# A two-layer hybrid encoder on one core: the second pair of differential heads moved to the end of the attention

## The chip, the core and the metric

The kernel runs on one NeuronCore of one Trainium2 chip. Its time is the device time of one execution in microseconds (us), and the number to be predicted is the median over several executions. TensorE (PE in the profile) multiplies matrices into eight PSUM banks; VectorE (DVE), ScalarE (ACT) and GpSimd (POOL) do everything else on tiles, and SyncE's queue (SP) starts all transfers. Each engine works through its own instructions strictly in the order in which the program lists them and waits where an operand isn't ready.

## What is computed

The reference, cut to one layer (512 tokens, width 1024, two layers, all in float32):

```python
for l in range(DEPTH):
    x = x + 0.5 * swiglu(rms_norm(x, ffn1_norm[l]), ...)
    h = rms_norm(x, mix_norm[l])
    pa, pb, pc, pd = jnp.split(h @ w_in[l], IN_SPLITS, axis=-1)
    ya = neighbourhood_mixer(pa, ...)   # 4 heads; a query sees 256 or 384 of the 512 keys here
    yb = mla_mixer(pb, ...)             # 4 heads behind two latent projections
    yc = diff_mixer(pc, ...)            # 4 heads, each softmax(1) - lam * softmax(2), plus T5 bias
    yd = gqa_mixer(pd, ...)             # 4 heads on 2 pairs of keys and values
    x = x + jnp.concatenate([ya, yb, yc, yd], axis=-1) @ w_out[l]
    x = x + 0.5 * swiglu(rms_norm(x, ffn2_norm[l]), ...)
    x = rms_norm(x, final_norm[l])
```

## The kernel before

Everything is kept transposed: 128 channels on the partitions, 512 tokens along a row. Every matrix product is done in three passes on numbers split into a high and a low part (`mm3`), so that one 128x128 block of weights against 512 tokens is three matmuls of 128x512. A layer is the first feed-forward block, the attention stage (`mix`), and the second feed-forward block.

In `mix` each group of heads (A neighbourhood, B latent, C differential, D grouped) has a projection (`proj_a`, `proj_b`, `proj_c`, `proj_d`; C and A in two halves "c0", "c1" and "a0", "a1", D in "d0" and "d1"), and its heads' attention is cut into steps of 128 queries, 64 steps a layer. A step writes score tiles into PSUM (one tile, or two in group C, whose heads have two softmaxes: 80 tiles a layer), reads each on DVE with the bias or for its maximum, takes the exponential on ACT, is transposed on TensorE back into PSUM, split on ACT and DVE, and every second step multiplies with the values. Scores alternate between two banks (ring "sc"), transposes between two others ("tr"), one bank collects values ("po"), and projections share two ("mm"). So score tile k+2 can't be written before DVE has read tile k.

After the last step of a group `finish` normalises its outputs and `commit` splits them into two of the eight tiles `xh`, `xl`. `out_proj` multiplies six of these with the output weights (18 matmuls for each of eight row blocks d, and one split of a 128x768 weight piece and one addition to `x[d]` on DVE), and what the last group adds follows in `out_proj_a`, six matmuls for each d. The order of steps is the list `units`; between steps a `Filler` hands out projection and output work in portions (`PACE`).

That order is only the input of a planner: `Plan.issue` takes all recorded operations, simulates them with costs and dependences (and with DVE and GpSimd operations that use their common port held apart), and sorts every engine's instructions by the start times that it found. All instructions therefore carry line L216 in the profile, and tiles must tell them apart: `bank` is PSUM, `round` and `plain` are two large arenas in SBUF, `kr` holds the identity and selection matrices, `x` the running sum.

Of the kernel before, what the change touches and what calls it, by code (L numbers as in the profile page):

```python
# [13 lines left out]
F32R = mybir.dt.float32r  # L14
# [6 lines left out]
P = 128  # L21
T = 512
# [6 lines left out]
ROWS = T // GRID_W  # L29

BANKS = {"mm": 2, "st": 1, "po": 1, "sc": 2, "tr": 2}
PACE = {"c0": 2.5, "c1": 2.5, "d0": 3.0, "d1": 3.0, "b": 3.0, "a0": 1.0, "a1": 1.0}

G_F1, G_MIX, G_F2, G_FIN = 0, 8, 16, 24
G_NAQ, G_NAK, G_NAB = 32, 33, 34
# [184 lines left out]
def tile_encoder(ctx: ExitStack, tc: tile.TileContext, xT, wf, wd, win, wout, wuq, wukv, gains, lamp, rpb, t5,  # L220
# [23 lines left out]
    def area(dt, at, n, rows=P):  # L244
        return arenas[dt][:rows, at:at + n]

    xh, xl = ([area(F32R, (at + 12 * T + k * T) if k < 2 else (k - 2) * T + off, T) for k in range(KD)]
              for at, off in ((32 * T, 0), (34 * T, 6 * T)))  # L250

    def krs(off, n, rows=P):
        return kr[:rows, off:off + n]
# [34 lines left out]
    def bank(tag):  # L288
        return rings[tag].take()
# [40 lines left out]
    def mm3(o, wh, wl, ah, al, first, last):  # L330
        TE.matmul(o, wh, ah, start=first, stop=False)
        TE.matmul(o, wh, al, start=False, stop=False)
        TE.matmul(o, wl, ah, start=False, stop=last)
# [3 lines left out]
    for i, tag in enumerate(("whi", "wlo")):  # L337
        rings[tag] = Ring([area(F32R, 48 * T + (2 * i + j) * 1024, 1024) for j in range(2)])

    def pieces(l):  # L340

        for i in range(20):
            yield win[l, (0, 1, 2, 3, 4, 5, 6, 8, 9, 7, 10, 11, 12, 13, 14, 15, 16, 17, 18, 19)[i]], 1024, G
            if i == 13:
                yield wuq[l], 768, G
                yield wukv[l], 512, G
        for d in range(KD):
            yield wout[l, d, :, 256:1024], 768, V
        for d in range(0, KD, 4):
            yield wout[l, d:d + 4, :, 0:256].rearrange("d p c -> p d c"), 1024, V  # L350
# [526 lines left out]
    def mix(l):  # L877
# [21 lines left out]
        def ring(tag):  # L899
            return mr[tag].take()  # L900
# [125 lines left out]
        class Group:  # L1026
# [7 lines left out]

            def head(self, h, o):
                if self.ys[h // 2] is None:
                    self.ys[h // 2] = ring("qf") if self.g == 0 else x[2 * (self.g - 1) + 1 + h // 2]
                t = ring("hs")
                S.copy(t[:64], o[64:128])
                r = 64 * (h % 2)  # L1040
                V.tensor_tensor(out=self.ys[h // 2][r:r + 64], in0=o[:64], in1=t[:64], op=ALU.add)
# [42 lines left out]

        def out_proj():

            for d in range(KD):
                hi, lo = weight()
                o = bank("mm")
                for i, k in enumerate((4, 5, 6, 7, 2, 3)):  # L1090
                    c = (k - 2) * P
                    mm3(o, hi[:, c:c + P], lo[:, c:c + P], xh[k], xl[k], i == 0, i == 5)
                    if i % 2:
                        yield 1.3
                DMA.dma_start(x[d], xd[d])
                V.tensor_tensor(out=x[d], in0=x[d], in1=o, op=ALU.add)
                yield 0.0

        def out_proj_a(ws):
            for d in (0, 4, 1, 5, 2, 6, 3, 7):  # L1100
                hi, lo = ws[d // 4]
                o = bank("ff")
                for k in range(2):
                    c = (d % 4 * 2 + k) * P
                    mm3(o, hi[:, c:c + P], lo[:, c:c + P], xh[k], xl[k], k == 0, k == 1)
                V.tensor_tensor(out=x[d], in0=x[d], in1=o, op=ALU.add)

        def transpose_p(pt_h, pt_l, p, col, nkt):
# [447 lines left out]
        def call(fn, *a):  # L1556
# [1 line left out]
            yield 0.6  # L1558

        units = [  # L1560
            ("c0", steps_c(C, 0, lambda: done["c0"])), ("c1", steps_c(C, 1, lambda: done["c1"])),
            ("d0", steps_d(Dg, 0, keep, lambda: done["d0"])), ("d1", steps_d(Dg, 1, keep, lambda: done["d1"])),
            ("b", steps_b(B, 0, lambda: done["b"])), ("b", steps_b(B, 1, lambda: done["b"])),
            ("a0", steps_a(A, 0, lambda: done["a0"])), ("a1", steps_a(A, 1, lambda: done["a1"])),
        ]
        ends = {15: (C, [gcs, gcs], True), 31: (Dg, [gcol(l, G_DB), gcol(l, G_DB + 1)], False),
                47: (B, [gcol(l, G_BB), gcol(l, G_BB + 1)], False), 63: (A, [gcol(l, G_NAB), gcol(l, G_NAB + 1)], False)}
        for name, gen in (("c0", proj_c(0, "sc")), ("c1", proj_c(1)), ("d0", proj_d(0, keep)), ("d1", proj_d(1, keep)), ("b", proj_b()),
                          ("a0", proj_a(0)), ("a1", proj_a(1))):
            fill.add(name, gen)  # L1570
        flat = [(u, st) for u, sts in units for st in sts]
        n = len(flat)
# [10 lines left out]
        for k in range(n + 1):  # L1583
            if k + 1 < n:
                flat[k + 1][1].soft()
            if k + 2 < n:
                begin(k + 2)
            if k < n:
                flat[k][1].trans()
            if k:  # L1590
                flat[k - 1][1].values()
                if k - 1 in ends:
                    g, beta, sub = ends[k - 1]
                    urgent.append((g, g.finish(beta, sub)))
            for it in list(urgent):
                more = next(it[1], "end")
                if more == "end":
                    urgent.remove(it)
                    if it[0] is not A:
                        fill.add("commit", call(it[0].commit))  # L1600
                    if it[0] is B:
                        fill.add("out", out_proj())
            if k < n:
                fill.run(PACE[flat[k][0]])
# [1 line left out]
            for _ in it[1]:  # L1606
                pass
        fill.until("out")
        A.commit()
        ws = [weight(), weight()]  # L1610
        ahead_ffn(l, 1)
        out_proj_a(ws)

    def start():

# [67 lines left out]
def _layout(inputs):  # L1683
    g = {k: np.asarray(v) for k, v in inputs.items()}
    L = g["w_in"].shape[0]
    xT = np.ascontiguousarray(g["x"][0].T.reshape(KD, P, T).transpose(1, 0, 2))
    wf, wd, win, wout, wuq, wukv, gains = [], [], [], [], [], [], []
    for l in range(L):
        f_, d_ = [], []
        for n in (1, 2):  # L1690
            a, b = _pieces(g[f"ffn{n}_w_gate"][l], P), _pieces(g[f"ffn{n}_w_up"][l], P)
            f_.append(np.stack([a, b], 1).reshape(-1, P, D))
            d_.append(_pieces(g[f"ffn{n}_w_down"][l], P))
        wf.append(np.stack(f_))
        wd.append(np.stack(d_))
        w = g["w_in"][l]
        A, B, C, Dg = w[:, :768], w[:, 768:1184], w[:, 1184:1952], w[:, 1952:]
        halves = [[m[:, 256 * i + P * p:256 * i + P * p + P] for p in range(2) for i in range(3)] for m in (C, A)]
        order = np.concatenate(halves[0] + [Dg, B[:, :384]] + [B[:, 384:]] * 4 + halves[1], axis=1)
        win.append(_pieces(order, P))  # L1700
        wout.append(_pieces(g["w_out"][l], P))
        q = g["mla_w_uq"][l].reshape(256, 4, 96)
        q = np.concatenate([q[:, :, :64].reshape(256, 256), q[:, :, 64:].reshape(256, 128)], axis=1)
        wuq.append(q.reshape(2, P, 384).transpose(1, 0, 2).reshape(P, 768))
        kv = g["mla_w_ukv"][l].reshape(128, 4, 128)
        wukv.append(np.concatenate([kv[:, :, :64].reshape(128, 256), kv[:, :, 64:].reshape(128, 256)], axis=1))

        def col(a):
            return a[l].reshape(-1, P).T

        def rep(a, n):
            return np.concatenate([a] * n)[:, None]

        q, k = g["mla_q_norm"][l], g["mla_k_norm"][l]
        gains.append(np.concatenate([
            col(g["ffn1_norm"]), col(g["mix_norm"]), col(g["ffn2_norm"]), col(g["final_norm"]),
            rep(g["na_q_norm"][l], 2), rep(g["na_k_norm"][l], 2), col(g["na_beta"]),
            col(g["mla_q_lat_norm"]), col(g["mla_kv_lat_norm"]),
            rep(q[:64], 2), rep(q[64:], 4), rep(k[:64], 2), rep(k[64:], 4), col(g["mla_beta"]),
            rep(g["diff_q_norm"][l], 4), rep(g["diff_k_norm"][l], 4), rep(g["diff_subln"][l], 2),  # L1720
            rep(g["gqa_q_norm"][l], 2), rep(g["gqa_k_norm"][l], 2), col(g["gqa_beta"])], axis=1))
    kc, rope, oh, mask = _constants()
    return {
        "xT": xT, "wf": np.stack(wf), "wd": np.stack(wd), "win": np.stack(win), "wout": np.stack(wout),
        "wuq": np.stack(wuq), "wukv": np.stack(wukv), "gains": np.stack(gains, 1),
        "lamp": np.broadcast_to(g["diff_lambda"].reshape(L, 1, P), (L, P, P)),
        "rpb": g["na_rpb"].reshape(L, 4, 465), "t5": g["t5_bias"],
        "kconst": kc, "krope": rope, "konehot": oh, "kmask": mask,
    }
# [21 lines left out]
```

## Time and profile before

| | |
|---|---|
| median of 3 runs | 2020.22 us (2017.6 to 2021.91) |
| the profiled execution | 2016.73 us, of which the span from first to last instruction is 2014.9 us |
| TensorE busy | 1984.0 us, 98% of the span |
| VectorE, ScalarE, GpSimd busy | 77%, 49%, 9% |
| granted TensorE clock, mean | 0.996 |

The profiled execution lies 3.5 us under the median. The attention stages run from about 346 to 633 us (layer 0) and 1340 to 1640 us (layer 1). A busy TensorE is read here from starts: where matmuls follow each other in constant steps, nothing waits.

### The profile page before, as it was taken

How to read it: one execution, taken by the hardware profiler on the slowest of the kernel's cores; microseconds unless marked ns; L12 is line 12 of the kernel's file. 1: busy time of each engine (PE TensorE's matmuls, PEld its weight loads, DVE VectorE, ACT ScalarE, POOL GpSimd, SP SyncE). 2: the span in 40 equal slices, each digit the busy share in tenths (PEclk: the TensorE clock that was granted, in tenths of full speed). 3: DMA queues.
4: the chain of work that ended last, by engine and by line, in shares of the span. 5: the costliest groups of instructions: out<-in, count | busy, mean ns of one | idle time of the engine just before them, and what ended most of it. 6: DMA issues, size and time to landing. Idle time of an engine off the chain costs nothing.

```text
span 2014.9 us, 30935 instructions
## 1 busy us (share of the span) xinstructions
PE 1984.0 (98%) x12072; PEld 1767.3 (88%) x12072; DVE 1552.6 (77%) x2553; ACT 993.3 (49%) x1575; POOL 186.3 (9%) x147
## 2 busy tenths in 40 slices
PE   7999999999999999999999999999999999999997
PEld 6989989888888998989899898988888889889896
DVE  8957758699887984856899495675998889759575
ACT  6533424577776642433554243345677755425232
POOL 0000021443200000000000000012431000000000
PEclk9999999999999999999999999999999999999998
DMA  4343445554344142241414224153633431423322
GB/s 156 116 127 129 133 144 165 162 165 119 102 114 142 50 146 75 78 141 65 136 64 135 75 79 142 63 181 110 169 103 92 128 113 64 140 70 126 105 79 68
DMA packets 90666, 230.12 MB, mean 114 GB/s; under 512 B 9844, under 2 KB 24820, under 8 KB 90520
## 3 DMA queue, kind: packets, MB, share of 16 engines
q1 hardware_dynamic: 90520, 228.15, 36.5%
q8 instruction: 95, 1.56, 0.3%
q14 instruction: 51, 0.42, 0.1%
HBM read 192.83 MB, written 14.27 MB: 103 GB/s over the span
## 4 chain that ended last, share of the span: by engine, by line
PE 91%; DVE 5%; DMA 2%; issue 1%; ACT 1%; SPq 0%; POOLq 0%; POOL 0%; DVEq 0%; ACTq 0%
PE bank L216 91%; DVE round L216 2%; DVE plain L216 2%; DMA plain<-in_wf_dram 1%; ACT round L216 1%; DMA plain<-in_win_dram 1%; DVE x L216 0%; DMA round<-nab 0%; DMA x<-in_xT_dram 0%; DMA plain<-in_wd_dram 0%; DMA xd<-x 0%; ACT plain L216 0%; SPq L216 0%; DVE dr L216 0%; DVE cc L216 0%
## 5 line engine op out<-in xcount | busy, mean ns | idle before, releaser
L216 PE MATMUL bank<-round 128*128 128x256 f32 (+3 forms) x10812 | 1893.9, 334 | 16.1 <-ACT round L216 11.8
L216 PEld LDWEIGHTS bank<-round 128*128 128x128 f32 (+1 forms) x10812 | 1625.5, 190 | 208.0 <-ACT round L216 11.9
L216 ACT CAST round<-plain 128x1024 fp32r<-128x1024 f32 (+2 forms) x576 | 541.2, 955 | 646.0 <-PE bank L216 406.4
L216 DVE TENSOR_TENSOR round<-plain,round 128x1024 fp32r<-128x1024 f32 (+2 forms) x532 | 582.2, 1114 | 106.9 <-ACT round L216 105.1
L216 DVE TENSOR_TENSOR plain<-plain 128x512 f32<-128x512 f32 (+2 forms) x442 | 294.0, 684 | 55.4 <-DMA plain<-in_wf_dram 32.0
L216 DVE TENSOR_TENSOR x<-x,bank 128x512 f32<-128x512 f32 x130 | 88.8, 685 | 159.7 <-PE bank L216 159.6
L216 ACT COPY plain<-bank 128x256 f32<-128x256 f32 (+2 forms) x240 | 97.0, 413 | 142.2 <-PE bank L216 91.3
L216 PEld LDWEIGHTS bank<-kr,plain 128*128 128x128 f32 x968 | 121.5, 164 | 17.4 <-DVE round L216 0.7
L216 PE MATMUL bank<-kr,plain 128*128 128x128 f32 (+3 forms) x968 | 132.2, 257 | 0.4 <-DVE plain L216 0.3
L216 POOL TENSOR_TENSOR round<-plain,round 128x1024 fp32r<-128x1024 f32 (+2 forms) x44 | 105.1, 2390 | 250.0 <-ACT round L216 201.3
L216 DVE TENSOR_TENSOR round<-bank,round 128x512 fp32r<-128x512 f32 (+4 forms) x162 | 103.5, 644 | 24.9 <-ACT round L216 23.7
L216 DVE TENSOR_TENSOR plain<-bank,plain 128x256 f32<-128x256 f32 (+2 forms) x200 | 101.7, 515 | 26.7 <-PE bank L216 16.8
L216 ACT CAST round<-bank 128x512 fp32r<-128x512 f32 (+4 forms) x162 | 87.7, 550 | 52.9 <-PE bank L216 51.5
L216 ACT ACTIVATE plain<-plain 128x1024 f32<-128x1024 f32 (+1 forms) x64 | 59.4, 928 | 64.7 <-DVE plain L216 64.1
L216 POOL TENSOR_TENSOR r<-z,mhalf 128x4 f32<-128x4 f32 (+1 forms) x7 | 9.2, 1320 | 803.2 <-DVE z L216 803.2
L216 ACT ACTIVATE plain<-plain,nm 128x512 f32<-128x512 f32 (+2 forms) x96 | 64.1, 669 | 21.0 <-DVE nm L216 20.4
L216 DVE CUSTOM_DVE_ANT_0 plain<-bank,round 128x512 f32<-128x512 f32 (+2 forms) x96 | 58.5, 617 | 9.7 <-PE bank L216 8.6
L216 DVE TENSOR_REDUCE mx<-bank 128x1 f32<-128x512 f32 x64 | 43.9, 685 | 7.5 <-PE bank L216 7.0
L216 POOL MEMSET round<- 128x128 f32 (+1 forms) x36 | 8.0, 240 | 405.1 <-PE bank L216 404.5
L216 POOL TENSOR_TENSOR plain<-plain 128x256 f32<-128x256 f32 (+1 forms) x24 | 26.4, 1127 | 156.0 <-DMA plain<-nad 156.0
L216 DVE TENSOR_TENSOR plain<-plain,R 128x1024 f32<-128x1024 f32 x32 | 39.1, 1222 | 0.5
L216 DVE SCALAR_TENSOR_TENSOR plain<-plain,R 128x1024 f32<-128x1024 f32 x32 | 39.1, 1221 | 0.4
(169 smaller groups left out, 679.9 us busy)
## 6 DMA issues: line engine op xcount, KB each, us to landing
plain<-in_wf_dram SPq DMA_DIRECT2D x176, 512.0 KB, 3.3
plain<-in_wd_dram SPq DMA_DIRECT2D x64, 512.0 KB, 4.0
plain<-in_win_dram SPq DMA_DIRECT2D x40, 512.0 KB, 3.4
round<-round SPq DMA_DIRECT2D x112, 128.0 KB, 2.5
plain<-in_wd_dram SPq DMA_DIRECT2D x32, 384.0 KB, 3.9
round<-round SPq DMA_DIRECT2D x40, 256.0 KB, 4.0
plain<-in_wout_dram SPq DMA_DIRECT2D x16, 384.0 KB, 2.9
xd<-x SPq DMA_DIRECT2D x16, 256.0 KB, 4.1
```

Of the source, the lines that this page charges most:

```text
L216: call(*a, **kw)
```

## The change

In `mix`, the second half of group C (its projection "c1" and its two heads) moves from second to last place, behind group A. Group A is no longer the last group, so `out_proj` now takes D, B and A and starts after A's commit; what the two last tiles add (`out_proj_c`) comes from group C. The tiles of C therefore take the places in the arena and the rows of the output weights that A had (`MIXED`, and the row order in the host's layout of `w_out`). The weight pieces come in the new order, A's heads collect in `x[4]` and `x[0]` and the first pair of C in `x[3]`; since `x[3]` is then read until C's commit, row block 3 comes last in `out_proj`, stays open in its bank, gets its last six matmuls there, and `x[3]` is loaded back only after the commit. The portions in `PACE` are different. The number of matmuls, score tiles and splits is the same.

```diff
-PACE = {"c0": 2.5, "c1": 2.5, "d0": 3.0, "d1": 3.0, "b": 3.0, "a0": 1.0, "a1": 1.0}
+PACE = {"c0": 2.5, "d0": 2.0, "d1": 2.0, "b": 2.0, "a0": 2.0, "a1": 2.0, "c1": 2.5}
...
+    MIXED = (4, 5, 0, 1, 2, 3, 6, 7)
+    xh, xl = ([area(F32R, (at + k * T) if k < 2 else (k - 2) * T + off, T) for k in map(MIXED.index, range(KD))]
+              for at, off in ((44 * T, 0), (46 * T, 6 * T)))
...
+    LAST = (0, 1, 2, 4, 5, 6, 7, 3)
...
+        for i in (0, 1, 2, 6, 8, 9, 7, 10, 11, 12, 13, 14, 15, 16, 17, 18, 19, 3, 4, 5):
+            yield win[l, i], 1024, G
...
         def out_proj():
-            for d in range(KD):
+            for d in LAST:
                 hi, lo = weight()
                 o = bank("mm")
-                for i, k in enumerate((4, 5, 6, 7, 2, 3)):
-                    c = (k - 2) * P
-                    mm3(o, hi[:, c:c + P], lo[:, c:c + P], xh[k], xl[k], i == 0, i == 5)
+                for i, k in enumerate((6, 7, 2, 3, 0, 1)):
+                    c = (MIXED.index(k) - 2) * P
+                    mm3(o, hi[:, c:c + P], lo[:, c:c + P], xh[k], xl[k], i == 0, i == 5 and d != LAST[-1])
                     if i % 2:
                         yield 1.3
+                if d == LAST[-1]:
+                    return o
                 DMA.dma_start(x[d], xd[d])
                 V.tensor_tensor(out=x[d], in0=x[d], in1=o, op=ALU.add)
...
-        def out_proj_a(ws):
+        def out_proj_c(ws, last):
+            free = Ring([b for b in banks[:6] if b is not last])
+            DMA.dma_start(x[LAST[-1]], xd[LAST[-1]])
...
         units = [
-            ("c0", steps_c(C, 0, lambda: done["c0"])), ("c1", steps_c(C, 1, lambda: done["c1"])),
+            ("c0", steps_c(C, 0, lambda: done["c0"])),
             ("d0", steps_d(Dg, 0, keep, lambda: done["d0"])), ("d1", steps_d(Dg, 1, keep, lambda: done["d1"])),
             ("b", steps_b(B, 0, lambda: done["b"])), ("b", steps_b(B, 1, lambda: done["b"])),
             ("a0", steps_a(A, 0, lambda: done["a0"])), ("a1", steps_a(A, 1, lambda: done["a1"])),
+            ("c1", steps_c(C, 1, lambda: done["c1"])),
         ]
...
-                    if it[0] is B:
+                    if it[0] is A:
                         fill.add("out", out_proj())
```

Three places show what the planner makes of it, all in the attention stage of layer 0. A row is a run of equal instructions, with its output, inputs and size.

TensorE in group A's attention, before: banks 82 and 83 get scores (128x256, 128x384), 84 and 85 transposes (128x128), 81 the values, and 78 and 79 (128x512) are the output projection.

```order
L216 MATMUL bank_79<-round 128x512 x3
L216 MATMUL bank_85<-kr,plain 128x128 x2
L216 MATMUL bank_78<-round 128x512
L216 MATMUL bank_79<-round 128x512
L216 MATMUL bank_83<-round 128x256 x2
L216 MATMUL bank_81<-round 128x256
L216 MATMUL bank_78<-round 128x512 x5
L216 MATMUL bank_84<-kr,plain 128x128 x2
L216 MATMUL bank_81<-round 128x256
L216 MATMUL bank_82<-round 128x384
L216 MATMUL bank_81<-round 128x256
L216 MATMUL bank_82<-round 128x384
```

The same engine in group A's attention now; bank 79 is here the last projection of c1.

```order
L216 MATMUL bank_81<-round 128x256 x3
L216 MATMUL bank_82<-round 128x256 x2
L216 MATMUL bank_81<-round 128x256 x3
L216 MATMUL bank_85<-kr,plain 128x128 x3
L216 MATMUL bank_81<-round 128x256
L216 MATMUL bank_83<-round 128x256 x2
L216 MATMUL bank_81<-round 128x256
L216 MATMUL bank_79<-round 128x512
L216 MATMUL bank_82<-round 128x384 x2
```

The matmuls of 128x512 between A's steps, ten of them in the first piece, are down to one in the second.

VectorE while the output projection runs, before (beside steps of group A): ISA is the read of a score tile with its bias, `round<-bank` the split of transposed scores, `round<-plain` of 128x768 the split of an output weight, `x<-x` an addition to the sum.

```order
L216 ISA plain,nm_1_0_149<-bank_83,round 128x256
L216 ISA nm_1_0_149 128x1
L216 ISA plain,nm_1_1_150<-bank_82,round 128x384
L216 ISA nm_1_1_150 128x1
L216 TENSOR_TENSOR plain<-bank_81,plain 64x512
L216 TENSOR_TENSOR round<-bank_85,round 128x3x128
L216 TENSOR_TENSOR round<-bank_84,round 128x3x128
L216 ISA plain,nm_1_2_151<-bank_83,round 128x384
L216 ISA nm_1_2_151 128x1
L216 TENSOR_TENSOR x<-x,bank_79 128x512
```

VectorE while the output projection runs now (beside steps of c1).

```order
L216 ISA plain,nm_0_125<-bank_83,round 128x512
L216 ISA nm_0_125 128x1
L216 ISA plain,nm_1_126<-bank_82,round 128x512
L216 ISA nm_1_126 128x1
L216 TENSOR_TENSOR x<-x,bank_78 128x512
L216 SCALAR_TENSOR_TENSOR cc_0_133<-cc_0_133,lam_0_112,ss_2_121 128x1
L216 TENSOR_TENSOR round<-bank_85,round 128x4x128
L216 TENSOR_TENSOR round<-plain,round 128x768
L216 SCALAR_TENSOR_TENSOR plain<-plain,cc_0_133 128x512
L216 ISA plain,nm_1_126<-bank_83,round 128x512
```

A step beside the output projection now reads two score tiles of full width where it read one of half or three quarters, and joins its two softmaxes (the 128x512 `plain<-plain,cc`).

TensorE from the last head's values (bank 81) on, now: `128x2` are the sums of `finish`, `4x128` the transposes of its factors, `round,kr` their spreading, the other 128x512 are the output projection.

```order
L216 MATMUL bank_81<-round 128x256 x8
L216 MATMUL bank_84<-kr,plain 128x2 x2
L216 MATMUL bank_78<-round 128x512 x9
L216 MATMUL bank_79<-round 128x512 x3
L216 MATMUL bank_84<-kr,plain 128x2 x4
L216 MATMUL bank_79<-round 128x512 x15
L216 MATMUL bank_78<-round 128x512 x6
L216 MATMUL bank_85<-kr,F_0_166 4x128 x4
L216 MATMUL bank_78<-round 128x512 x8
L216 MATMUL bank_84<-round,kr 128x512
L216 MATMUL bank_85<-round,kr 128x512
L216 MATMUL bank_78<-round 128x512 x4
```

Behind these rows stand 24 more of the output projection (bank 79 x18, bank 78 x6), and then `out_proj_c`. So 69 matmuls of the output projection stand behind the last values.

## Rows read from the trace of the kernel before

**Rows 1.** The page: span, and each engine's busy time, share of the span, instructions.

```profile
span 2014.9 us, 30935 instructions
...
PE 1984.0 (98%) x12072; PEld 1767.3 (88%) x12072; DVE 1552.6 (77%) x2553; ACT 993.3 (49%) x1575; POOL 186.3 (9%) x147
```

**Rows 2.** Busy time by stretch: PE, PEld, DVE, ACT, POOL; then clock, DMA share, GB/s.

```profile
346.00:633.00 287.00, 285.76 (x1660) 246.31 (x1659) 240.74 (x571) 190.81 (x382) 77.83 (x55) 1.00 0.46 131
520.00:580.00 60.00, 60.00 (x379) 52.54 (x379) 52.03 (x116) 45.34 (x92) 8.63 (x4) 1.00 0.33 84
...
1340.00:1640.00 300.00, 296.65 (x1694) 253.99 (x1693) 244.95 (x575) 192.69 (x383) 72.67 (x52) 0.99 0.44 126
1430.00:1460.00 30.00, 29.69 (x162) 25.01 (x161) 29.65 (x66) 21.25 (x44) 14.75 (x8) 1.00 0.76 206
1360.00:1368.00 8.00, 5.32 (x22) 4.39 (x22) 2.52 (x8) 5.82 (x10) 0.76 (x1) 0.79 0.12 43
```

**Rows 3.** Who TensorE waited for: us in total, times, longest.

```profile
PE bank L216 <- DVE R L216: 2.7, 1, 2.7
```

**Rows 4.** Groups by shape, TensorE, 520 to 580 us: count | busy, mean ns | idle before.

```profile
L216 PE MATMUL bank<-round 128*128 128x512 f32 x91 | 26.5, 404 | 0.0
L216 PE MATMUL bank<-round 96*128 96x512 f32 x48 | 15.5, 413 | 0.0
L216 PE MATMUL bank<-round 128*128 128x256 f32 x89 | 14.6, 288 | 0.0
L216 PE MATMUL bank<-kr,plain 128*128 128x128 f32 x88 | 13.7, 272 | 0.0
```

**Rows 5.** TensorE in order of time, two long runs: start, us, what, count.

```profile
633.21 41.19 PE L216 MATMUL bank<-round 128*128 128x512 f32 x181
...
680.62 52.62 PE L216 MATMUL bank<-round 128*128 128x256 f32 x435
```

**Rows 6.** VectorE in order of time, two dense pieces: start, us, what.

```profile
424.97 0.16 DVE L216 RECIPROCAL cc<-s 128x1 f32<-128x1 f32 x1
425.04 0.67 DVE L216 TENSOR_TENSOR round<-bank,round 128x512 fp32r<-128x512 f32 x1
...
427.81 0.21 DVE L216 SCALAR_TENSOR_TENSOR cc<-cc,lam,ss 128x1 f32<-128x1 f32 x1
427.94 0.68 DVE L216 TENSOR_TENSOR round<-plain,round 128x512 fp32r<-128x512 f32 x1
428.54 0.74 DVE L216 SCALAR_TENSOR_TENSOR plain<-plain,cc 128x512 f32<-128x512 f32 x1
429.20 0.68 DVE L216 TENSOR_TENSOR round<-plain,round 128x512 fp32r<-128x512 f32 x1
...
605.13 0.96 DVE L216 TENSOR_TENSOR round<-plain,round 128x768 fp32r<-128x768 f32 x1
606.01 0.42 DVE L216 TENSOR_TENSOR round<-bank,round 128x256 fp32r<-128x256 f32 x1
606.34 0.42 DVE L216 CUSTOM_DVE_ANT_0 plain<-bank,round 128x256 f32<-128x256 f32 x1
...
606.68 0.56 DVE L216 CUSTOM_DVE_ANT_0 plain<-bank,round 128x384 f32<-128x384 f32 x1
...
607.16 0.68 DVE L216 TENSOR_TENSOR plain<-bank,plain 64x512 f32<-64x512 f32 x1
```

**Rows 7.** All engines in order of time, start of the second attention stage.

```profile
1354.10 2.40 POOL L216 TENSOR_TENSOR round<-plain,round 128x1024 fp32r<-128x1024 f32 x1 [8.49 <-DVE lv L216]
...
1354.59 2.45 DVE L216 TENSOR_TENSOR R<-R,plain 128x512 f32<-128x512 f32 x1 [0.56 <-ACT plain L216]
...
1362.69 1.05 PE L216 MATMUL bank<-ones,R 128*128 128x1 f32 x8 [2.68 <-DVE R L216]
```

**Rows 8.** SyncE's queue: 16 copies of score operands; transfers by kind, KB, us to landing.

```profile
394.31 10.63 SPq L216 DMA_DIRECT2D round<-round  x16
...
round<-round SPq DMA_DIRECT2D x112, 128.0 KB, 2.5
```

More of the change, by code (lines that the diff above doesn't have):

```diff
@@ L245, in area @@
         return arenas[dt][:rows, at:at + n]
-    xh, xl = ([area(F32R, (at + 12 * T + k * T) if k < 2 else (k - 2) * T + off, T) for k in range(KD)]
-              for at, off in ((32 * T, 0), (34 * T, 6 * T)))
+    MIXED = (4, 5, 0, 1, 2, 3, 6, 7)
+    xh, xl = ([area(F32R, (at + k * T) if k < 2 else (k - 2) * T + off, T) for k in map(MIXED.index, range(KD))]
+              for at, off in ((44 * T, 0), (46 * T, 6 * T)))
     def krs(off, n, rows=P):
@@ L338, in tile_encoder @@
         rings[tag] = Ring([area(F32R, 48 * T + (2 * i + j) * 1024, 1024) for j in range(2)])
+    LAST = (0, 1, 2, 4, 5, 6, 7, 3)
     def pieces(l):
-        for i in range(20):
-            yield win[l, (0, 1, 2, 3, 4, 5, 6, 8, 9, 7, 10, 11, 12, 13, 14, 15, 16, 17, 18, 19)[i]], 1024, G
+        for i in (0, 1, 2, 6, 8, 9, 7, 10, 11, 12, 13, 14, 15, 16, 17, 18, 19, 3, 4, 5):
+            yield win[l, i], 1024, G
             if i == 13:
@@ L1085, in out_proj @@
         def out_proj():
-            for d in range(KD):
+            for d in LAST:
                 hi, lo = weight()
                 o = bank("mm")
-                for i, k in enumerate((4, 5, 6, 7, 2, 3)):
-                    c = (k - 2) * P
-                    mm3(o, hi[:, c:c + P], lo[:, c:c + P], xh[k], xl[k], i == 0, i == 5)
+                for i, k in enumerate((6, 7, 2, 3, 0, 1)):
+                    c = (MIXED.index(k) - 2) * P
+                    mm3(o, hi[:, c:c + P], lo[:, c:c + P], xh[k], xl[k], i == 0, i == 5 and d != LAST[-1])
                     if i % 2:
                         yield 1.3
+                if d == LAST[-1]:
+                    return o
                 DMA.dma_start(x[d], xd[d])
@@ L1097, in out_proj @@
                 yield 0.0
-        def out_proj_a(ws):
+        def out_proj_c(ws, last):
+            free = Ring([b for b in banks[:6] if b is not last])
+            DMA.dma_start(x[LAST[-1]], xd[LAST[-1]])
             for d in (0, 4, 1, 5, 2, 6, 3, 7):
                 hi, lo = ws[d // 4]
-                o = bank("ff")
+                o = last if d == LAST[-1] else free.take()
                 for k in range(2):
                     c = (d % 4 * 2 + k) * P
-                    mm3(o, hi[:, c:c + P], lo[:, c:c + P], xh[k], xl[k], k == 0, k == 1)
+                    mm3(o, hi[:, c:c + P], lo[:, c:c + P], xh[MIXED[k]], xl[MIXED[k]], k == 0 and d != LAST[-1], k == 1)
                 V.tensor_tensor(out=x[d], in0=x[d], in1=o, op=ALU.add)
@@ L1564, in mix @@
             ("a0", steps_a(A, 0, lambda: done["a0"])), ("a1", steps_a(A, 1, lambda: done["a1"])),
+            ("c1", steps_c(C, 1, lambda: done["c1"])),
         ]
[L1566 to L1569, printed above, removed]
+        ends = {23: (Dg, [gcol(l, G_DB), gcol(l, G_DB + 1)], False), 39: (B, [gcol(l, G_BB), gcol(l, G_BB + 1)], False),
+                55: (A, [gcol(l, G_NAB), gcol(l, G_NAB + 1)], False), 63: (C, [gcs, gcs], True)}
+        for name, gen in (("c0", proj_c(0, "sc")), ("d0", proj_d(0, keep)), ("d1", proj_d(1, keep)), ("b", proj_b()),
+                          ("a0", proj_a(0)), ("a1", proj_a(1)), ("c1", proj_c(1))):
             fill.add(name, gen)
@@ L1598, in mix @@
                     urgent.remove(it)
[L1599 removed]
+                    if it[0] is not C:
                         fill.add("commit", call(it[0].commit))
[L1601 removed]
+                    if it[0] is A:
                         fill.add("out", out_proj())
@@ L1608, in mix @@
         fill.until("out")
-        A.commit()
+        C.commit()
         ws = [weight(), weight()]
         ahead_ffn(l, 1)
-        out_proj_a(ws)
+        out_proj_c(ws, done["out"])
     def start():
@@ L1700, in _layout @@
         win.append(_pieces(order, P))
-        wout.append(_pieces(g["w_out"][l], P))
+        wout.append(_pieces(g["w_out"][l].reshape(KD, P, D)[[4, 5, 0, 1, 2, 3, 6, 7]].reshape(D, D), P))
         q = g["mla_w_uq"][l].reshape(256, 4, 96)
```

2 lines of the change are left out of this document (1 added, 1 removed).

## The prediction

> **What bounds the kernel now.** I read the page first. TensorE is busy for 1984.0 of 2014.9 us [rows 1], so at most 31 us can be won in the whole program, and a change in the attention can win only what TensorE loses there. The busy time by stretch says how much that is: in the first attention stage 285.76 of 287.00 us are busy, in the second 296.65 of 300.00 [rows 2]. That is 1.2 and 3.4 us. The list of waits names the largest piece of the second: 2.7 us, once, for VectorE's tile R [rows 3], at the start of the stage. So the attention is bound by TensorE's own work, and what has to be asked of the change is whether TensorE still finds work everywhere. VectorE is the engine that could stop it: 240.74 of 287 us in the first stage, and 29.65 of 30 between 1430 and 1460 us, where TensorE nevertheless ran for 29.69 [rows 2], because it had projections to do beside the scores.
>
> **Prices.** For both engines I take the step from one start to the next where work is dense. TensorE: 181 matmuls of 128x512 in 41.19 us and 435 of 128x256 in 52.62 [rows 5], less the last one's own tail, give 0.227 and 0.121 us; 128x384 I put midway, 0.174. From 520 to 580 us TensorE is busy without a gap with 379 matmuls [rows 2]: 146 are 512 wide (91 and 48 [rows 4], and seven in a smaller group), 89 are 256 wide [rows 4], and 144 are small (88 transposes [rows 4] and 56 others). 60.00 - 146 x 0.227 - 89 x 0.121 leaves 16.1 us, so 0.112 for a small one. VectorE [rows 6]: 0.60 us for a tensor-tensor of 512 (427.94 to 428.54), 0.66 for the scalar form (428.54 to 429.20), 0.88 for 768 (605.13 to 606.01), 0.33 for 256, 0.34 and 0.48 for reads of score tiles of 256 and 384 (606.34, 606.68). A read of 512 I take as 0.60, a split of 384 as 0.48. Small ones run from 0.07 (424.97) to 0.13 (427.81); I take 0.10.
>
> **The change part by part.** Removed and added work cancel: as many matmuls, score tiles, splits and transfers as before. What counts is what stands beside what. TensorE needs for a step of group A about 0.95 us and VectorE about as much (read, split, part of a head's sum); for a step of group C TensorE needs two scores, four transposes and half of eight value products, 2 x 0.227 + 4 x 0.112 + 4 x 0.121 = 1.4 us, while VectorE needs two reads, the joining of the softmaxes, a split and small things, 3 x 0.60 + 0.66 + 0.3 = 2.8 us. Only filler from projections or from the output projection lets TensorE stay busy beside that. An output block d is such filler: 18 x 0.227 = 4.1 us of TensorE against 0.88 + 0.60 = 1.5 us of VectorE.
>
> Before, all 16 steps of A ran beside the output projection. Now they run without it, since it needs A's commit, and have only the last projection of c1; the steps of c1 have the output projection, but its first blocks come late. I count this in layer 0's order. A score bank is free again only when VectorE has read the tile in it, so tile k+2 waits for the read of tile k. From the ninth score tile of A (tile 57 of 80) to the read of c1's eleventh (75), VectorE has in its queue: 12 reads of 512, 22 tensor-tensor of 512, 8 scalar forms, 2 of 768, 10 of 384, 4 reads and 5 splits of 256, and 21 small ones: 7.2 + 13.2 + 5.3 + 1.8 + 4.8 + 3.0 + 2.1 = 37.4 us. TensorE has between tile 57 and tile 77, which waits for that read, 82 matmuls of 512, 8 of 384, 59 of 256 and 65 small ones: 18.6 + 1.4 + 7.1 + 7.3 = 34.4 us. So TensorE must stand for 2.9 us there at least. The same count over the old last stretch (from A's first tile to the tile that waits for its thirteenth) gives TensorE 58, 14, 52 and 52 matmuls, 27.7 us, and VectorE 24.2 us; there TensorE never waited. Layer 1's order has the same counts to within 0.1 us.
>
> To the 2.9 us come handovers at both ends: a matmul of 256 lasts 0.288 us and takes a slot of 0.121 [rows 4, 5], an operation of VectorE ends 0.08 us after its slot (0.68 against 0.60 [rows 6]); with the signals I take 0.4. Second, GpSimd: the last two weight pieces of c1 are split there between B's finish and A's second pair of heads. At 1354.10 such a split ran for 2.40 us, and VectorE's addition beside it, with both inputs in SBUF, took 2.45 instead of 0.60 [rows 7]. One of the two pieces falls into the stretch or just ahead of it: between 0 and 1.85 us, and I take 1.1, somewhat over the middle, because the pieces last longer than any one operation of VectorE and so meet several of them. [...] Third, the queue of SyncE: c1's 16 copies of score operands now stand late in the stage, behind two bias loads and ahead of the reloads of x. Sixteen took 10.63 us to issue and each 2.5 to land [rows 8], so the eight that the first step of c1 needs take 8 x 0.66 + 2.5 = 7.8 us; VectorE has 14 operations, 6.7 us, to do meanwhile. That exposes 0 to 1.1 us; I take 0.2, since the second half of the stack isn't needed at once.
>
> The end is covered. Behind the last values stand 69 matmuls of the output projection, 15.7 us, in the pieces 12, 21, 8 and 28. The longest link is the last: 28 x 0.227 = 6.4 us against two scalings (1.3), the two splits of the commit (1.2) and an addition and a weight split between them (about 1.8). Were this cover gone, up to 15.7 us a layer would come to light. The late reload of `x[3]` waits for the commit on SyncE, with 17 weight loads of the next block queued behind it; it has six blocks, 36 x 0.227 = 8.2 us, to land, twice the data of the 2.5 us above, so at most 5 us. The weights behind it land after that, before the next block has used its first pair.
>
> Sum for a layer: 2.9 + 0.4 + 1.1 + 0.2 = 4.6 us, for two layers 9.2. Against it 0.3 us that TensorE lost at 1430 to 1460 us [rows 2] beside c1's steps go away. So +9 us: the profiled execution's 2016.73 becomes 2025.7, and with the 3.5 us by which the median of the runs shown lies above it, 2029.2.
>
> **The rivals.** *The second stage starts better.* The wait of 2.7 us [rows 3] comes from GpSimd's split in front of the addition to R [rows 7]; behind it the clock stood at a mean of 0.79 for 8 us [rows 2], which is 3.4 us at 1.2 GHz and 1.7 us lost. The order of this place is nearly the same as before (16 projection matmuls stand ahead of the sums in both), which speaks against it, but some of the splits around it are exchanged. If they fall otherwise, 4.4 us come back: 2024.8, and 2022 with the smallest shortage of 2 x 2.9 + 0.8.
>
> *Faster.* Sixteen score tiles of C leave the first third of the stage, where VectorE and GpSimd are in each other's way (29.65 and 14.75 of 30 us [rows 2]). All that TensorE could win in both stages is 1.2 + 3.4 + 1.7 = 6.3 us: 2013.9. It decides only if the shortage is under 1.1 us a layer, so if VectorE's prices are 5% too high; against that stands that they are steps of back-to-back operations.
>
> *The clock falls.* The waits in the new stretch are some tenths of a microsecond each, again and again over 40 us. One fall costs 1.7 us as above; with one or two in each layer the time is 2029.2 + 3.4 to 6.8, about 2034. For it speaks that the low clock from 1360 us on came with a wait of TensorE, though one of 2.7 us at a stretch; against it that between 1430 and 1460 us, with 0.3 us of waits, the clock stayed at 1.00 [rows 2]. The Trainium skill (TensorE: Matmul & The Clock Gate, A second HAM failure mode: psum-queue depth-cycling) describes a kernel whose TensorE idles briefly between groups of matmuls as it cycles through PSUM banks, and whose clock then goes back and forth; that is this rival, and no row of this case shows it so far.
>
> **How the numbers follow.** VectorE's shortage as counted: 0.65. Its own range: two layers of 3.3 less 0.3, +6.3 us, up to 3.3 + 2 x 1.85 + 1.1 = 8.1 a layer, +16: 2026.5 to 2036.4. The better start: 0.15; faster: 0.06; the clock: 0.14. About 0.2% (4 us) is what the measurement can tell from no change. Slower by more than that are the first and the last case and a good part of the second: 0.82; within it most of the rest, 0.12; faster 0.06. For 8 in 10 the range begins inside the better start, at 2021.5, and ends in the clock's case, at 2036.5.
>
> **What would show it.** Right: TensorE's busy time in both attention stages falls short of the stage by 4 to 8 us more than before, in the last 60 us of the stage; the waits there name VectorE's reads and splits; VectorE is busy there without gaps. No waits behind the last head's values, and none for `x[3]`. Wrong: no gaps in TensorE there (the prices or the counting of the banks fail), gaps that name a transfer `round<-round` (the copies of c1), gaps of single microseconds with a clock under 1.00, or a start of the second stage without its wait.

## The result, and the profile after

| | before | after |
|---|---|---|
| median | 2018.91 us (4 runs, 2017.05 to 2021.91) | 2046.99 us (4 runs, 2043.73 to 2048.88) |
| ratio | | 1.0142 (95%: 1.0124 to 1.0161) |
| TensorE busy, of the span | 1984.0 of 2014.9 us [rows 1] | 2004.4 of 2044.8 us |

The change costs 28 us, where 9 were forecast: the direction was right, and the time lies outside the range of 2021.5 to 2036.5. The page of the changed kernel, against [rows 1]:

```profile
span 2044.8 us, 30951 instructions
...
PE 2004.4 (98%) x12072; PEld 1777.4 (87%) x12072; DVE 1548.8 (76%) x2551; ACT 992.6 (49%) x1575; POOL 183.8 (9%) x147
```

The same 12072 matmuls are busy for 20 us more, so much of the loss isn't idle time. The mean granted clock accounts for part of it: 0.990 where it was 0.996, and 0.006 of 2044.8 us is 12 us.

To split the loss by stage I take marks that both kernels have: a long run of 128x256 matmuls in the first feed-forward block, and in each second feed-forward block the run of eight `kr,hl` matmuls behind the attention. The kernel before, TensorE in order of time (start, us, what):

```profile
311.94 33.45 PE L216 MATMUL bank<-round 128*128 128x256 f32 x230 [0.50 <-DVE round L216]
...
679.77 1.00 PE L216 MATMUL bank<-kr,hl 128*128 128x128 f32 x8
...
1674.34 1.00 PE L216 MATMUL bank<-kr,hl 128*128 128x128 f32 x8
```

The changed kernel, the same view and the same three marks:

```profile
311.05 34.33 PE L216 MATMUL bank<-round 128*128 128x256 f32 x233 [0.50 <-DVE round L216]
...
694.24 1.00 PE L216 MATMUL bank<-kr,hl 128*128 128x128 f32 x8
...
1703.59 1.00 PE L216 MATMUL bank<-kr,hl 128*128 128x128 f32 x8
```

Over layer 0's attention 367.83 us became 383.19 (+15.4), and from there over layer 1's 994.57 became 1009.35 (+14.8). That is the whole 30 us between the two spans, half in each layer. Inside the stages, by windows (columns as in [rows 2]):

```profile
430.00:450.00 20.00, 18.98 (x91) 16.10 (x90) 14.25 (x27) 10.64 (x21) 7.50 (x4) 0.74 0.55 154
...
438.00:449.00 11.00, 10.86 (x40) 9.43 (x41) 5.60 (x11) 2.03 (x6) 3.30 (x3) 0.53 0.58 162
440.00:449.00 9.00, 8.96 (x29) 7.64 (x30) 3.60 (x8) 1.90 (x5) 2.50 (x2) 0.50 0.49 143
479.00:484.00 5.00, 5.00 (x30) 4.96 (x30) 2.99 (x2) 2.45 (x6) 2.76 (x2) 0.66 0.25 72
...
600.00:624.00 24.00, 21.98 (x115) 16.33 (x115) 23.29 (x62) 17.04 (x38) 1.01 (x1) 1.00 0.69 192
...
1440.00:1460.00 20.00, 17.28 (x87) 14.48 (x85) 13.94 (x27) 10.42 (x21) 7.59 (x4) 0.83 0.66 162
...
1449.00:1456.00 7.00, 6.69 (x21) 5.66 (x22) 2.85 (x6) 1.63 (x4) 1.76 (x2) 0.51 0.64 180
1524.00:1528.00 4.00, 3.94 (x15) 2.94 (x16) 1.58 (x4) 0.26 (x1) 0.00 (x0) 0.57 0.07 17
...
1610.00:1634.00 24.00, 22.55 (x120) 16.89 (x119) 23.86 (x63) 17.83 (x39) 1.01 (x1) 1.00 0.71 197
```

The windows at 600 and 1610 us are the forecast stretch, where VectorE is busy for 23.3 and 23.9 of 24 us. Those at 430 and 1440 us lie where c0 gives way to d0, in the first third of the stage. There VectorE is less busy than TensorE, and the clock has a mean of 0.74 and 0.83. The prediction has no cost for that place.

A matmul's record is longer than its slot and hides part of each gap, so I price the windows as the prediction did, by counts of matmuls. TensorE's groups by shape, changed kernel, 600 to 624 us:

```profile
L216 PE MATMUL bank<-round 128*128 128x512 f32 x51 | 15.2, 417 | 1.4 <-DVE nm L216 0.8 <-DMA round<-round 0.6
L216 PE MATMUL bank<-kr,plain 128*128 128x128 f32 x22 | 3.5, 278 | 0.5 <-DVE cc L216 0.5
L216 PE MATMUL bank<-round 128*128 128x256 f32 x20 | 3.3, 298 | 0.0
L216 PE MATMUL bank<-kr,plain 128*128 128x2 f32 x16 | 1.9, 241 | 0.0
L216 PE MATMUL bank<-round,kr 128*128 128x512 f32 x2 | 0.9, 452 | 0.1
L216 PE MATMUL bank<-kr,F 128*4 128x128 f32 x4 | 0.6, 272 | 0.0
```

53 x 0.227 + 20 x 0.121 + 42 x 0.112 = 19.15 us of work in 24: 4.85 us lost. From 1610 to 1634 us five more matmuls of 128x512 stand, so 3.7 are lost. The same view from 430 to 450 us:

```profile
L216 PE MATMUL bank<-round 128*128 128x512 f32 x33 | 12.3, 503 | 0.5 <-DVE round L216 0.4
L216 PE MATMUL bank<-kr,plain 128*128 128x128 f32 x19 | 3.4, 305 | 0.0
L216 PE MATMUL bank<-round 128*128 128x256 f32 x15 | 3.2, 337 | 0.0
L216 PE MATMUL bank<-kr,plain 128*128 128x1 f32 x16 | 2.9, 306 | 0.0
L216 PE MATMUL bank<-kr,plain 128*128 128x2 f32 x8 | 1.1, 254 | 0.5 <-DVE round L216 0.5
```

33 x 0.227 + 15 x 0.121 + 43 x 0.112 = 14.1 us of work in 20: 5.9 us lost, and 6.2 by the same count from 1440 to 1460 us. The rest is at the start of group B in layer 1 (a wait of 2.4 us and the low clock of the window at 1524, 1.7), the low clock at 479 (1.7), and single waits. So of 30 us the end of the stages has 8.6, the change from c0 to d0 12.0, group B's start 4.1 and the fall at 479 us 1.7; 3.6 us are not placed.

What happens at that change, changed kernel, all engines in order of time:

```profile
431.01 0.68 DVE L216 CUSTOM_DVE_ANT_0 plain<-bank,round 128x512 f32<-128x512 f32 x1
...
431.62 0.69 DVE L216 TENSOR_TENSOR round<-plain,round 128x512 fp32r<-128x512 f32 x1
...
431.97 2.59 POOL L216 TENSOR_TENSOR round<-plain,round 128x1024 fp32r<-128x1024 f32 x1 [8.47 <-ACT round L216]
...
432.29 2.30 DVE L216 TENSOR_SCALAR d0n<-dr 128x16 f32<-128x16 f32 x1
...
434.51 0.68 DVE L216 TENSOR_TENSOR round<-plain,round 128x512 fp32r<-128x512 f32 x1
...
435.21 3.48 SPq L216 DMA_DIRECT2D round<-round  x4
...
435.97 1.55 PE L216 MATMUL bank<-kr,plain 128*128 128x2 f32 x12 [0.51 <-DVE round L216]
...
437.89 0.50 PE L216 MATMUL bank<-round 128*128 128x512 f32 x1 [0.37 <-DVE round L216]
...
440.04 2.26 PE L216 MATMUL bank<-round 128*128 128x512 f32 x5
```

The read at 431.01 is c0's last. Only behind it does VectorE split d0's queries (431.62) and keys (434.51), and only then are the keys copied (435.21 to 438.69); d0's first scores start at 440.04. TensorE meanwhile waits for VectorE at 435 and 437 us, runs matmuls of one and two columns, and its clock falls: from 440 to 449 us it is busy without a break at 0.50, the lower of its two levels. Two explanations offered themselves: GpSimd's split at 431.97 holds VectorE's tiny operation at 432.29 for 2.30 us and makes everything late ("port"); or the work around c0 is simply in the wrong order or out of cover ("cover").

### The profile page after: what moved, and what is told of

Its sections match the earlier page's. It is cut to its first block, busy times and chain, and to the rows that moved or that the text cites. A ratio compares the mean times of both kernels' runs of the same rounds, so it can differ in the third digit from the quotient of the medians.

```text
span 2044.8 us, 30951 instructions
## 1 busy us (share of the span) xinstructions
PE 2004.4 (98%) x12072; PEld 1777.4 (87%) x12072; DVE 1548.8 (76%) x2551; ACT 992.6 (49%) x1575; POOL 183.8 (9%) x147
## 4 chain that ended last, share of the span: by engine, by line
PE 79%; DVE 14%; DMA 4%; issue 2%; ACT 1%; POOL 0%; SPq 0%; DVEq 0%; POOLq 0%; ACTq 0%
PE bank L216 79%; DVE round L216 6%; DVE plain L216 5%; DMA plain<-in_wf_dram 2%; DMA round<-round 1%; DVE x L216 1%; DMA plain<-in_win_dram 1%; ACT round L216 1%; DVE R L216 0%; DVE cc L216 0%; DVE rt L216 0%; POOL r L216 0%; DVE rb L216 0%; DVE zb L216 0%; DMA x<-in_xT_dram 0%
## 5 line engine op out<-in xcount | busy, mean ns | idle before, releaser
L216 PE MATMUL bank<-round 128*128 128x256 f32 (+2 forms) x10812 | 1907.8, 335 | 26.5 <-ACT round L216 10.5
```

The lines of the kernel that those rows point to most:

```text
L216: call(*a, **kw)
```

## The experiments

**1. The four splits at the change from c0 to d0 (e1), all splits (e2), and all in the kernel before (e3).** The order of every engine is kept; at the moment of issue GpSimd's subtraction becomes a memset:

```diff
+            k = -1
             for _, i in order:
                 call, a, kw = ops[i][2], *ops[i][4:6]
+                if ops[i][0] == 2 and kw.get("op") == ALU.subtract and kw["out"].dtype == F32R:
+                    k += 1
+                    if k in (7, 8, 9, 10, 29, 30, 31, 32):      # e2, e3: range(44)
+                        self.tc.nc.gpsimd.memset(kw["out"].bitcast(F32), 0.0)
+                        continue
                 call(*a, **kw)
```

> The changed kernel with every engine's order kept, but four of GpSimd's weight splits in each attention stage (the ones at 418.8, 421.1, 432.0 and 436.4 us and their counterparts in layer 1) are replaced by a memset of the low part to zero, so the low part of these four weight pieces is left out. Theory 'port': these splits lock VectorE at the change from c0 to d0 (1.7 + 1.7 + 2.1 + 0.8 us), TensorE runs dry behind that and the clock falls; without them the waits at 435 to 440 us and the low clock behind them go, about 6.5 us a layer, and the time is about 2034. Theory 'cover': VectorE has more to do there than TensorE in any case since c1's projection no longer stands beside it; the gaps stay and the time is 2044 to 2047.

> The changed kernel with every order kept and all 44 of GpSimd's weight splits replaced by memsets (the low part of the attention's weights is left out). Port: besides the 13 us at the change from c0 to d0 also the start of the second stage (4.3 us), the start of group B in layer 1 (4.2) and some single gaps (about 2) come back: about 2023, of which some 9 us over the kernel before are the shortage at the end of the stages, which stays at 600 to 621 and 1610 to 1630 us. Cover: 2038 to 2043, only the start of the second stage comes back.

> The kernel before with every order kept and all 44 of GpSimd's weight splits replaced by memsets (low part left out). Both theories: TensorE hardly waited in it, so only the wait for R at the start of the second stage (2.7 us) and the low clock behind it (1.7) come back: about 2014.5. The difference to the changed kernel without its splits is then what the change costs without the port: 9 to 10 us by 'port', 25 or more by 'cover'.

Measured: e1 2045.26 us (1.0133 of before, 1.0106 to 1.0160), e2 2039.33 (1.0102, 1.0076 to 1.0128), e3 2013.12 (0.9978, 0.9966 to 0.9989). "Port" falls: it forecast about 2034 for e1, which gave back under 2 us by the medians, and without any of the splits the change still costs 2039.33 - 2013.12 = 26.2 us, as "cover" had it. What e1 shows from 430 to 450 us:

```profile
430.00:450.00 20.00, 18.09 (x92) 15.82 (x91) 11.33 (x27) 10.29 (x20) 4.41 (x4) 0.74 0.56 154
```

92 matmuls where there were 91, and the same clock. GpSimd no longer holds VectorE up, and what TensorE waits for now is the copies themselves (waits of TensorE in e1, 425 to 450 us: us, times, longest):

```profile
PE bank L222 <- DMA round<-round: 1.9, 1, 1.9
```

In e2 TensorE reaches d0's first scores sooner, at 436.43 instead of 440.04 us, and waits for the copies there too (e2, 425 to 447 us):

```profile
PE bank L222 <- DMA round<-round: 1.6, 1, 1.6
```

**2. The portions of before in the new order (e4).**

```diff
-PACE = {"c0": 2.5, "d0": 2.0, "d1": 2.0, "b": 2.0, "a0": 2.0, "a1": 2.0, "c1": 2.5}
+PACE = {"c0": 2.5, "d0": 3.0, "d1": 3.0, "b": 3.0, "a0": 1.0, "a1": 1.0, "c1": 2.5}
```

> The changed kernel with the portions of before (3.0 for D and B, 1.0 for A, 2.5 for both halves of C); the planner makes a new order of it. If the smaller portions for D and B are what leaves TensorE without work at the change from c0 to d0, the gaps at 435 to 440 us go and the time falls to 2030 to 2035. If it is the place of c1 that matters, the time stays within 5 us of 2047, and the gaps are at about the same place.

2049.33 us (1.0133, 1.0094 to 1.0171): the portions that the change altered aren't the cause. In this order d0's two splits stand behind c0's 14th and 16th read, nothing on VectorE is held up between them, and in layer 0 TensorE waits 1.7 us for the copies, with a mean clock of 0.76 from 430 to 450 us.

**3. d0's projection recorded earlier beside c0 (e7), and c1 between d1 and b (e6).** e7 is the changed kernel with one number altered:

```diff
-PACE = {"c0": 2.5, "d0": 2.0, "d1": 2.0, "b": 2.0, "a0": 2.0, "a1": 2.0, "c1": 2.5}
+PACE = {"c0": 6.0, "d0": 2.0, "d1": 2.0, "b": 2.0, "a0": 2.0, "a1": 2.0, "c1": 2.5}
```

> The changed kernel with one number different: the portion of filler behind each step of c0 is 6.0 instead of 2.5, so that d0's projection is recorded early in c0's steps. In VectorE's order the two splits of d0's operands then stand behind c0's 8th and 13th score read, where in the changed kernel they stand behind the 16th, the last. Theory 'late operands': TensorE stands at 435 to 440 us because d0's queries and keys are made and copied only when c0 has nothing left; with the early order these gaps and the low clock behind them go, 6 to 6.5 us a layer, and the time is 2032 to 2036. Rival 'too little TensorE work': VectorE has more to do than TensorE in c0's whole stretch now that c1's projection isn't there; then the gaps only move forward into c0's steps and the time stays at 2043 to 2049.

2030.31 us (1.0055, 1.0038 to 1.0072): 16.7 us of the medians come back by this number. TensorE at the change from c0 to d0, e7, layers 0 and 1 (d0's first row maximum is at 449.18 us, its copies were issued from 432.90 to 440.48):

```profile
430.00:455.00 25.00, 25.00 (x149) 21.61 (x147) 17.42 (x53) 15.23 (x31) 8.80 (x6) 1.00 0.53 149
1435.00:1460.00 25.00, 25.00 (x147) 21.52 (x147) 17.85 (x53) 15.22 (x31) 8.30 (x7) 1.00 0.56 152
```

No gap and full clock: the last of d0's copies is issued 8.7 us before its first row maximum. "Late operands" stands, and it is a matter of order: no work was added or removed. "Too little TensorE work" falls, since the gaps didn't move forward: TensorE waits for nothing from 400 to 460 us. But the planner's whole order is new, and not all of the 16.7 us belongs to this place: the wait of 2.4 us at group B's start in layer 1 is gone as well, and the one for `x` at the start of the second stage has grown from 2.4 to 4.6 us.

e6 is the kernel before with c1 moved only behind d1 (A stays last):

```diff
-            ("c0", steps_c(C, 0, lambda: done["c0"])), ("c1", steps_c(C, 1, lambda: done["c1"])),
+            ("c0", steps_c(C, 0, lambda: done["c0"])),
             ("d0", steps_d(Dg, 0, keep, lambda: done["d0"])), ("d1", steps_d(Dg, 1, keep, lambda: done["d1"])),
+            ("c1", steps_c(C, 1, lambda: done["c1"])),
```

(`ends`, the order of the projections and that of the weight pieces follow.)

> The kernel before with c1 between d1 and b: its steps no longer stand between c0 and d0, but A stays last beside the output projection, with the portions of before. d0's operand splits stand behind the 13th and 15th of c0's 16 reads. 'Late operands': gaps of 1 to 2.5 us at the change from c0 to d0 in each layer, with a fall of the clock behind them: 2021 to 2029, and no gaps in the last 40 us of the stages. If all of the change's cost came from the end of the stages, it would be within 3 us of the kernel before.

2020.44 us against 2018.53 (1.0010, 1.0000 to 1.0019): less than expected. In layer 0 nothing is lost at the change (420 to 445 us):

```profile
420.00:445.00 25.00, 25.00 (x143) 21.07 (x142) 24.42 (x61) 14.62 (x30) 9.76 (x5) 1.00 0.69 197
```

In layer 1 a wait of 0.7 us stands there, with a low clock behind it (mean 0.77 from 1425 to 1440 us). So c1 can leave its place between c0 and d0 for 2 us in all, when d0's operands are split behind c0's 13th and 15th read as here. With the same portions and the second split behind the 16th read, e4 had the loss; so one to three reads seem to make the difference, though e6 differs from e4 in more than that (A stays last).

**4. The end of the stage (e9, e10, e11).** e9 leaves out the splits of the output weights on VectorE:

```diff
+                if ops[i][0] == 0 and kw.get("op") == ALU.subtract and kw["out"].dtype == F32R and kw["out"].shape[-1] == 768:
+                    continue
                 call(*a, **kw)
```

> The changed kernel with every order kept, without VectorE's eight splits of 128x768 output-weight pieces a layer (the low part of these weights is left out, the old content of the tile is used). If VectorE's shortage makes the waits at 600 to 621 and 1610 to 1630 us (5.2 and 4.2 us), the two splits that lie in that stretch give back 0.9 us each: 1.5 to 3.5 us in both layers, so 2043 to 2045, and the sum of TensorE's gaps there falls to 2.5 to 3.5 us a layer. If the waits there come from signals between engines or from the copies, they stay, and the time is 2047.

2047.11 us (1.0139, 1.0124 to 1.0155): nothing, which is what the rival (signals or copies) forecast. But the experiment was aimed badly and doesn't decide. In the changed kernel one of these splits stands ahead of the stretch's waits in each layer, at 601.37 and 1611.96 us, and the next come behind the last of them, at 624.66 and 1634.33. e10 and e11 take away what does stand between the waits, in e7's order:

```diff
                         V.scalar_tensor_tensor(out=rowmajor(yn), in0=colmajor(ys[j]), scalar=beta[j], in1=colmajor(o), op0=ALU.mult, op1=ALU.mult)
+                        plan.skip.add(len(plan.ops) - 1)        # e10, e11: not issued
...
                 V.scalar_tensor_tensor(out=sb[0], in0=sb[1], scalar=cc, in1=sb[0], op0=ALU.mult, op1=ALU.add)
+                if self.hd.h >= 2:
+                    plan.skip.add(len(plan.ops) - 1)            # e11 alone
```

> The changed kernel with the portion 6.0 for c0 (2030.3 us), its order kept, but without the two scalings of 128x512 with which VectorE finishes group A in the last stretch of each attention stage (1.1 us each; A's outputs are left unnormalised). In the profile of that kernel TensorE's waits at 605 to 610 and 1608 to 1613 us (2.9 us a layer) stand just around these two. If VectorE's work is what is short there, they fall by 2 us or more a layer and the time to 2025 to 2027; if signals and bank turns make the waits, they fall by under 0.5 us a layer: 2029 to 2031.

> As e10, and also without the joining of the two softmaxes in c1's eight steps a layer (128x512 on VectorE, 0.66 us each; one softmax is left out of these heads). VectorE short: the waits in the last stretch are gone but for the one for c1's copies (0.5 us), 2022 to 2025. Signals and bank turns: 2028 to 2031.

e10 2028.86 us (1.0040, 1.0024 to 1.0057), e11 2026.25 (1.0035, 1.0022 to 1.0048). The times don't decide: e10 lies just under the rival's 2029 to 2031 and not at 2025 to 2027, e11 lies between the two forecasts, and the steps between the medians, 1.5 and 2.6 us (3.0 and 1.0 by the ratios), are smaller than the scatter. The windows say more. The last stretch of both layers, e7:

```profile
590.00:614.00 24.00, 22.15 (x116) 16.26 (x115) 23.40 (x63) 17.09 (x38) 1.01 (x1) 1.00 0.74 190
1590.00:1614.00 24.00, 22.56 (x123) 17.05 (x122) 23.84 (x63) 18.89 (x43) 1.17 (x3) 1.00 0.72 194
```

e10:

```profile
590.00:614.00 24.00, 22.84 (x125) 17.66 (x123) 23.24 (x64) 18.43 (x43) 1.01 (x1) 1.00 0.75 200
1590.00:1614.00 24.00, 23.23 (x129) 18.08 (x128) 23.40 (x64) 18.90 (x44) 1.01 (x1) 1.00 0.73 201
```

e11:

```profile
590.00:614.00 24.00, 23.15 (x132) 18.34 (x132) 21.75 (x62) 19.72 (x46) 1.52 (x5) 1.00 0.74 201
1590.00:1614.00 24.00, 23.88 (x136) 19.12 (x135) 22.46 (x64) 20.71 (x47) 1.01 (x1) 1.00 0.74 200
```

What TensorE lacks of 48 us falls from 3.29 to 1.93 to 0.97 us, and it gets through 239, 254 and 268 matmuls. So VectorE's work is the limit there, by the windows and not by the times. In e11 VectorE is no longer full, and the only wait left in layer 0 is the one for c1's copies (e11, waits of TensorE, 588 to 616 us):

```profile
PE bank L217 <- DMA round<-round: 0.7, 1, 0.7
```

**5. Can it be had for less? (e12, e8)** e12 is the changed kernel with 6.0 for c0, 4.0 for A, and the second weight piece split on VectorE; e8 is the kernel before with that last edit alone (shown as it stands in e12):

```diff
-            yield win[l, i], 1024, G
+            yield win[l, i], 1024, V if i == 1 else G
```

> The changed kernel with the portions 6.0 for c0 and 4.0 for A (so that c1's projection comes earlier beside A's steps) and the second weight piece of the stage split on VectorE; nothing left out. Late operands and the start of the second stage both mended, the shortage at the end only moved: 2021 to 2027, still above the kernel before (2016 to 2019). If the shortage at the end came from c1's late projection and copies rather than from VectorE's work, it would fall to 2017 to 2020.

> The kernel before with the second weight piece of each attention stage split on VectorE instead of GpSimd (nothing left out). VectorE's addition to R at the start of the second stage then isn't held up for 1.85 us by GpSimd's split; if that addition is what TensorE waits for there, the 2.7 us and the low clock behind them (1.7 us) go: 2012 to 2014 against 2016.4. If the split itself is what stands in the way, VectorE now does it in 1.1 us ahead of the addition and only about 1 us is won.

e12 2026.56 us (1.0039, 1.0026 to 1.0052): above the kernel before, as expected. These portions don't set the shortage at the end aside (from 590 to 614 us TensorE is busy for 21.28 us, and now waits there for VectorE alone); others were not tried. e8 2015.63 against 2018.53 (0.9990, 0.9981 to 1.0000): the best version of the study that leaves nothing out, by no more than can be measured. The wait for R fell from 2.7 to 1.7 us only, since the split that then comes next on GpSimd locks another small operation ahead of R (e8, start of the second stage):

```profile
1354.42 2.40 POOL L216 TENSOR_TENSOR round<-plain,round 128x1024 fp32r<-128x1024 f32 x1 [30.34 <-ACT round L216]
1354.74 2.14 DVE L216 TENSOR_TENSOR lv<-plain 128x32 f32<-128x32 f32 x1 [2.40 <-DMA plain<-in_lamp_dram]
```

## Why the prediction was wrong

**The step that failed** is the first sentence of "the change part by part": that removed and added work cancel, and that then only the stretch from A's ninth score tile on had to be counted. What stands beside what had changed at both ends of c1's move, and the cost was counted at one. The place that c1 left enters the prediction only as a gain: 0.3 us taken off the sum, and the rival *Faster*, as a relief for VectorE (29.65 of 30 us before [rows 2]). It cost 12.0 us: d0's operands came behind c0's last read, TensorE waited, and its clock fell. In e7, where they come earlier, nothing is lost in these two windows. The order of the changed kernel on VectorE had the two splits behind the 16th read before any run; the three places shown with the change don't include it.

**VectorE's shortage and the handovers, 3.3 us a layer:** right in place and cause, as the windows of e10 and e11 show. Of the measured 4.85 and 3.7 us, 0.6 in layer 0 belong to the copies; 4.2 and 3.7 remain. The sum priced A's two scalings of 128x512 at 0.66 us from start to start. Each took 0.96 (VectorE, changed kernel):

```profile
616.90 1.13 DVE L216 SCALAR_TENSOR_TENSOR plain<-x,gn,bank 128x512 f32<-128x512 f32 x1
617.86 0.17 DVE L216 RECIPROCAL cc<-s 128x1 f32<-128x1 f32 x1
```

The second ran from 618.51 to 619.47. These 0.6 us more lift 3.3 to 3.9. The code reads and writes these two in a permuted order (`rowmajor`, `colmajor`); whether that makes them longer was not tried.

**GpSimd, 1.1 us:** nothing. c1's last two pieces were split at 569.0 and 576.1 us, and TensorE's first wait of the stretch came at 604.9. **SyncE's copies, 0.2 us:** 0.6 in layer 0 (`DMA round<-round` in the rows by shape), none in layer 1; inside the bounds. **The end is covered**, with no wait for the last values or for `x[3]`: right. Together the terms made 9.2 us for two layers, and 8.6 were measured there; that they agree so well is partly luck, since 2.2 us for GpSimd that didn't come stand against scalings priced too low.

**The second stage's start** kept its price, against that rival: TensorE waited 2.4 us for `x`, where it was 2.7 for R, with a low clock behind it again.

**The clock** was a rival at 2034, with falls of 1.7 us in the stretch at the end. At the end the clock never fell, in spite of seven waits of 0.28 to 0.59 us. It fell at the front, for 11 us in layer 0 (mean 0.53) and 7 in layer 1 (0.51), and twice more. (1 - 0.53) x 11 + (1 - 0.51) x 7 + 1.7 + 1.7 = 12.0 us is an upper bound for what it took, with the waits inside these windows in it. So the low clock is up to 40% of the loss, and at the change from c0 to d0 it is up to 8.6 of the 12.0 us: the waits there are short, and most of their price is the clock behind them. Whether the waits at 435 and 437 us brought it down or the narrow matmuls between them was not separated.

**Group B's start**, 4.1 us in layer 1 and a few tenths in layer 0 with the same order: TensorE waited for copies (`DMA round<-round`, 2.4 us). Its first matmul of the group came 4.3 us after the last four, of 256 KB, began to be issued in layer 0, with a wait of 0.2 us, and 6.9 us after it in layer 1; why they landed later there was not tried.

What stays open is why the planner puts d0's splits behind c0's 13th and 15th read in e6, behind the 14th and 16th in e4 and both behind the 16th in the changed kernel, though all three record the same work up to there.

## What to carry to other kernels

A block that moves leaves a hole as well as making a crowd: count both places, and at the hole ask first when the next block's operands are ready, through to the landing of their copies. Here the late operands cost more than the shortage of work (12.0 against 8.6 us), and one number that moves their preparation a few steps forward, and other things with it, returned 16.7 of 28 us. When a suspected lock is plain in the trace (2.30 us on a tiny operation), take it away before believing in it: here the four splits were worth under 2 us.

## What the runs showed of the hardware

A VectorE operation of 128x16 with one input, `d0n<-dr`, took 2.30 us beside GpSimd's split of 2.59 us, and 0.15 in e1, where the split is a memset:

```profile
431.33 0.15 DVE L222 TENSOR_SCALAR d0n<-dr 128x16 f32<-128x16 f32 x1
```

So the lock isn't confined to operations with two tensors in SBUF, like the addition in [rows 7]. The Trainium skill (SBUF — State Buffer, Who interferes with whom) lists `tensor_scalar` among the operations that can take the port pair that VectorE and GpSimd share. This row agrees.

The clock can fall without a wait that the trace shows. In e3 TensorE was busy without a gap from 370 to 388 us and the list of waits is empty there, and yet (e3, windows):

```profile
370.00:378.00 8.00, 8.00 (x49) 7.01 (x48) 0.90 (x6) 5.96 (x9) 1.90 (x2) 1.00 0.20 68
378.00:388.00 10.00, 10.00 (x43) 8.37 (x43) 3.05 (x26) 1.09 (x3) 0.00 (x0) 0.66 0.16 52
```

Between 376 and 380 us it ran matmuls of one and four columns almost alone, and of the two levels, 1.2 and 2.4 GHz, the lower one followed. At the change from c0 to d0, too, the fall comes behind a group of matmuls of one and two columns, while at the end of the stage more and longer waits among matmuls of 512 columns left the clock at 1.00. Narrow matmuls alone don't settle it either: in e7 sixteen of one column in a row, 1.84 us from 434.82 us on, left it at 1.00. The Trainium skill (TensorE: Matmul & The Clock Gate, A second HAM failure mode: psum-queue depth-cycling) ties such falls to short idle times between groups of matmuls; this case has a fall without them (e3) and idle times without a fall (the end of the stage).
